# Stores of the gates, of FF1's first products and of its blocks and sums, issued by ScalarE and GpSimd in place of SyncE

## The chip, the core and the metric

The kernel runs on one core of a Trainium2 chip. The metric is the device time of one execution in microseconds (us). Every run compared here is one launch of the whole program. The engines are named as the profile names them: PE is TensorE, DVE is VectorE, ACT is ScalarE, POOL is GpSimd and SP is SyncE, which computes nothing and only issues transfers (DMAs).

## What is computed

One block of a streaming encoder, in fp32, for 1024 positions of width 1024:

```python
mod = silu(c) @ W_ada + b_ada                 # shift, scale, gate: twice
h = rms_norm(x) * (1 + scale1) + shift1
z = h @ W_in      # latents of q and kv, rotary key, input of the conv, 2 x 1024 gate logits
y_A = attention(z) @ W_o_mla                  # 8 heads, block-causal
y_B = conv_module(z)                          # GLU, depthwise conv (31), LayerNorm, swish, pointwise
x += gate1 * ((sigmoid(g_A) * y_A + sigmoid(g_B) * y_B) @ W_out)
h2 = rms_norm(x) * (1 + scale2) + shift2
x += gate2 * (relu(h2 @ W1) ** 2 @ W2)        # feed-forward, width 4096
```

## The kernel before

Each fp32 operand of a product is split into a high and a low part (`split`: a copy that rounds, mostly on ACT at line 108, then a subtraction on DVE or POOL at line 114), and each product is three matmuls (`mm`, line 117): high by high, low by high, high by low.

The stages, by the times of the profiled execution: adaLN, norm and h until 75 us; the GLU, the conv and the gates from 75 to 290; latents, keys and queries to 440, with the last gates between them; attention to 625; its output product to 700; W_out, the second norm and FF1's "first blocks" to 835; FF1's main loop to 1090; FF2 to the end.

Three groups of results that the change touches go to DRAM and back:

- The **gates** (`gate`, lines 405 to 409): each of the 16 blocks of 128 logits is a product of PE; ACT takes the sigmoid of each half from PSUM into a tile `sg`, and the half is stored to DRAM: 32 stores of 256 KB.
- FF1's **first products** (`first_block`, lines 1025 to 1032). FF1 is done by blocks with seven products where a plain 2 by 2 block scheme has eight. Products 1 and 2 of a block row m are computed ahead of the others for 12 of the 16 m. Product 1 is copied by ACT into a tile `p` and stored (`p1d`); product 1 plus product 2 is the block f11, which goes through ReLU and square on ACT (lines 1006 and 1007) and is stored (`fd`).
- FF1's **blocks and sums**. The main loop runs over the 16 m. For each, `prepare_w` loads two weight tiles p and q of 512 KB (line 891, tile `wraw`, two buffers for p) and forms sums and differences of their halves on DVE (lines 973, 974, 985, 986) and their splits (ACT: `hi`, `whi`, `s4h`; DVE: `lo`, `wlo`, `s4l`). PE runs products 3 to 7, DVE adds them up out of PSUM (`sum_of`, line 1015, tiles `u`), ACT squares f12, f21 and f22. `right_operands` (lines 1034 to 1050) loads f11 again (line 1037) and forms, on POOL, four sums T3, T1, T2, T4 (lines 1040, 1042, 1045, 1049), which FF2 needs as right operands. `keep` (line 1011) stores f22, f21 and the four sums: six stores of 256 KB for each m.

All 751 DMAs of the kernel are issued by SP, in one order. A framework builds that order, and the order of each engine, from the code and from its own forecast of the times; buffers and semaphores are its work too. An instruction waits where it stands for what it needs; what stands behind it on the same engine waits with it. So a store at the head of SP's queue, whose data is not there yet, holds the loads behind it.

Of the kernel before, what the change touches and what calls it, by code (L numbers as in the profile page):

```python
# [75 lines left out]
def block_kernel(ctx: ExitStack, tc: tile.TileContext, a: dict, out: bass.AP):  # L76
    nc = tc.nc
# [22 lines left out]
    def cs(c):  # L100
        return slice(c * C, (c + 1) * C)
# [4 lines left out]
    def copy(eng, o, i):  # L106
        if eng is nc.scalar:
            eng.activation(o, i, AF.Copy)  # L108
        else:
            eng.tensor_copy(o, i)  # L110
# [49 lines left out]
    d = first[4]  # L160
# [234 lines left out]
    def z_tile():  # L395
        return gemm(weights(), halves(h_hi), halves(h_lo), KD)

    s_d = [dram.tile([P, S], F32, name=f"sg{d}") for d in range(2 * KD)]
# [5 lines left out]
    def gate(d, new):  # L404
        o = z_tile()
        for c in range(2):
            s_t = new("sg")
            nc.scalar.activation(s_t, o[c], AF.Sigmoid)  # L408
            nc.sync.dma_start(s_d[d][:, cs(c)], s_t)

    def gates(n, new):
        for d in range(first[n], first[n + 1]):
            gate(d, new)
# [4 lines left out]
    with tc.tile_pool(name="cv", bufs=1, **right) as cv:  # L418
# [48 lines left out]
        for d in range(GA):  # L467
            gate(d, cv_half)
        conv(2, us[2])
        for d in range(GA, FILL[0]):  # L470
            gate(d, cv_half)
# [81 lines left out]
    with tc.tile_pool(name="lat", bufs=1, **left) as lat:  # L553
# [138 lines left out]
        d = first[4]  # L692
# [146 lines left out]
    def big(name, dt=F32):  # L839
# [4 lines left out]
    f_d = {n: [dram.tile([P, C], F32, name=f"fd{n}_{t}") for t in range(FF // P // 2)]  # L844
           for n in ("11", "21", "22", "T1", "T2", "T3", "T4")}
# [149 lines left out]
    def product(n, w):  # L995
        wk, bk = PRODUCTS[n]
        wh, wl = w[wk]
        o = bank()
        for i, (bh, bl) in enumerate(gb_[bk]):
            mm(o, wh[:, blk(i)], bh, i == 0, False)  # L1000
            mm(o, wh[:, blk(i)], bl, False, False)
            mm(o, wl[:, blk(i)], bh, False, i == 3)
        return o

    def square_relu(f):
        nc.scalar.activation(f, f, AF.Relu)  # L1006
        nc.scalar.activation(f, f, AF.Square)
        return f

    def keep(n, m, t):  # L1010
        nc.sync.dma_start(f_d[n][m], t)

    def sum_of(x, y):
        t = small("u")
        last_sum[0] = nc.vector.tensor_tensor(t, x, y, ALU.add)  # L1015
        return t

    p1 = {}
    last_sum = [None]
    p1_d = [dram.tile([P, C], F32, name=f"p1d{m}") for m in range(NPRE)]  # L1020

    def p1_tile(name):
        return small_pool.tile([P, C], F32, name=name, tag="p1", bufs=NP1)

    def first_block(m, w):
        p1[m] = p1_tile("p1")
        copy(nc.scalar, p1[m], product(1, w))
        if m < NPRE:
            nc.sync.dma_start(p1_d[m], p1[m])
        u = sum_of(product(2, w), p1[m])  # L1030
        keep("11", m, square_relu(u))
        return last_sum[0]

    def right_operands(m, f12, f21, f22):

        f11 = p1_tile("f11")
        nc.sync.dma_start(f11, f_d["11"][m])
        keep("22", m, f22)
        t3 = p1_tile("t3")
        nc.gpsimd.tensor_tensor(t3, f22, f12, ALU.subtract)  # L1040
        keep("T3", m, t3)
        nc.gpsimd.tensor_tensor(f12, f12, f11, ALU.subtract)
        keep("T1", m, f12)
        t2 = p1_tile("t2")
        nc.gpsimd.tensor_tensor(t2, f22, f12, ALU.subtract)
        keep("T2", m, t2)
        keep("21", m, f21)
        t4 = p1_tile("t4")
        nc.gpsimd.tensor_tensor(t4, f21, t2, ALU.subtract)
        keep("T4", m, t4)  # L1050

    NP = FF // P // 2
    rest = right_blocks()
# [1 line left out]
    for m in range(NPRE):  # L1055
        sums.append(first_block(m, first_row(m)[1]))
        if m >= 3:
            with tc.issue_after(sums[m - 1].ins):
                for _ in range(2):
                    next(rest, None)  # L1060
# [3 lines left out]
    for m in range(NP):  # L1064
        nxt = prepare_w(m + 1) if m + 1 < NP else None
        if m >= NPRE:
            first_block(m, w)
        if m == NP - 1:
            gap.close()
            w2a = ctx.enter_context(tc.tile_pool(name="w2a", bufs=1, **left))  # L1070
        ps = {n: product(n, w) for n in ((5, 3, 6, 7, 4) if m == 0 else (6, 7, 5, 3, 4))}
        if m < NPRE:
            p1[m] = small_pool.tile([P, C], F32, name="p1r")
            nc.sync.dma_start(p1[m], p1_d[m])
        u2 = sum_of(ps[6], p1[m])
        u3 = sum_of(ps[7], u2)
        f22 = square_relu(sum_of(ps[5], u3))
        u4 = sum_of(ps[5], u2)
        f12 = square_relu(sum_of(ps[3], u4))
        f21 = square_relu(sum_of(ps[4], u3))  # L1080
        right_operands(m, f12, f21, f22)
        w = nxt
# [222 lines left out]
```

## Time and profile before

| | |
|---|---|
| median of three runs | 1402.04 us (1401.58 to 1405.19) |
| the profiled execution: its own time | 1403.63 us |
| its span in the profile | 1401.5 us |
| PE busy | 1335.7 us, 95% of the span |
| DVE, ACT, POOL busy | 71%, 49%, 29% |
| DMA queue of SP | 49.3% of 16 engines' span |

The span is the time from the first to the last instruction that the profile shows; the execution's own time is 2.1 us longer. PE is the engine to watch: what does not lengthen or shorten its 66 us of idle time does not move the end. The engines' shares are means over stages that differ, so each place of the change has to be read by itself.

### The profile page before, as it was taken

How to read it: one execution, taken by the hardware profiler on the slowest of the kernel's cores; microseconds unless marked ns; L12 is line 12 of the kernel's file. 1: busy time of each engine (PE TensorE's matmuls, PEld its weight loads, DVE VectorE, ACT ScalarE, POOL GpSimd, SP SyncE). 2: the span in 40 equal slices, each digit the busy share in tenths (PEclk: the TensorE clock that was granted, in tenths of full speed). 3: DMA queues.
4: the chain of work that ended last, by engine and by line, in shares of the span. 5: the costliest groups of instructions: out<-in, count | busy, mean ns of one | idle time of the engine just before them, and what ended most of it. 6: DMA issues, size and time to landing. Idle time of an engine off the chain costs nothing. (4 is left out here: it accounts for less than half of the span.)

```text
span 1401.5 us, 17857 instructions
## 1 busy us (share of the span) xinstructions
PE 1335.7 (95%) x6160; PEld 1088.4 (78%) x6160; DVE 995.6 (71%) x1488; ACT 680.4 (49%) x1107; POOL 402.2 (29%) x280
## 2 busy tenths in 40 slices
PE   3899999999998999999999999989999999999998
PEld 2687888887676888878788878767778887887787
DVE  7969997955346788767546788766675459848854
ACT  6345422246556777753345763343455444444342
POOL 0049932244554655425100003334333100000000
PEclk9999999999999999999999999999999999999999
DMA  9611227731475323127546555566656678633442
GB/s 358 218 45 53 84 93 277 260 121 60 137 253 188 121 91 121 47 77 259 190 135 205 188 186 208 197 195 210 211 176 234 236 227 279 215 98 90 140 139 76
DMA packets 106186, 234.72 MB, mean 167 GB/s; under 512 B 12016, under 2 KB 12272, under 8 KB 106096
## 3 DMA queue, kind: packets, MB, share of 16 engines
q1 hardware_dynamic: 106096, 233.58, 49.3%
q8 instruction: 48, 0.79, 0.2%
q14 instruction: 42, 0.34, 0.1%
HBM read 169.57 MB, written 63.96 MB: 167 GB/s over the span
## 5 line engine op out<-in xcount | busy, mean ns | idle before, releaser
L117 PE MATMUL z<-hhi,whi 128*128 128x512 f32 x384 | 152.7, 399 | 0.4 <-ACT sg L408 0.4
L117 PE MATMUL z<-hlo,whi 128*128 128x512 f32 x384 | 152.4, 397 | 0.0
L117 PE MATMUL z<-hhi,wlo 128*128 128x512 f32 x384 | 152.1, 397 | 0.0
L1040 POOL TENSOR_TENSOR t<-u 128x512 f32<-128x512 f32 x16 | 23.0, 1440 | 316.4 <-DMA wraw<-in_w_ff 171.4
L108 ACT ACTIVATE whi<-wraw 128x1024 fp32r<-128x1024 f32 x71 | 74.9, 1055 | 59.7 <-PE z L117 46.4
L453 DVE SCALAR_TENSOR_TENSOR k<-u,vec,k 128x1024 f32<-128x1024 f32 x84 | 100.9, 1281 | 0.0
L114 POOL TENSOR_TENSOR wlo<-wraw,whi 128x1024 fp32r<-128x1024 f32 x25 | 62.6, 2503 | 115.0 <-ACT whi L108 110.3
L117 PEld LDWEIGHTS z<-hhi,whi 128*128 128x128 f32 x384 | 72.3, 188 | 19.6 <-ACT sg L408 1.0
L117 PEld LDWEIGHTS z<-hhi,wlo 128*128 128x128 f32 x384 | 72.3, 188 | 18.2
L117 PEld LDWEIGHTS z<-hlo,whi 128*128 128x128 f32 x384 | 72.4, 188 | 17.4
L114 DVE TENSOR_TENSOR wlo<-wraw,whi 128x1024 fp32r<-128x1024 f32 x46 | 60.7, 1319 | 26.2 <-ACT whi L108 26.2
L282 DVE CUSTOM_DVE_ANT_0 wada<-wada,c_act,vec 128x1024 f32<-128x1024 f32 x48 | 66.0, 1410 | 7.8 <-DMA wada<-in_w_ada 7.8
L1006 ACT ACTIVATE u<-u 128x512 f32<-128x512 f32 x64 | 39.9, 628 | 63.1 <-DVE u L1015 61.2
L446 POOL TENSOR_TENSOR accp<-accp,prc 128x1024 f32<-128x1024 f32 x28 | 67.4, 2413 | 9.8 <-ACT prc L445 8.6
L117 PE MATMUL z<-ghT,hi 128*128 128x512 f32 x160 | 62.9, 393 | 1.7 <-DVE u L1015 1.7
L117 PE MATMUL z<-glT,hi 128*128 128x512 f32 x160 | 62.5, 391 | 0.0
L117 PE MATMUL z<-ghT,lo 128*128 128x512 f32 x160 | 62.3, 390 | 0.0
L117 PE MATMUL z<-l_whi,h_whi 128*128 128x512 f32 x148 | 57.9, 391 | 4.1 <-DVE l_whi L114 4.1
L1015 DVE TENSOR_TENSOR u<-z,u 128x512 f32<-128x512 f32 x80 | 52.9, 684 | 10.4 <-PE z L117 7.2
L117 PE MATMUL z<-l_wraw,h_wraw 128*128 128x512 f32 x152 | 59.6, 392 | 0.0
L117 PE MATMUL z<-h_wraw,l_wraw 128*128 128x512 f32 x152 | 59.2, 390 | 0.0
L117 PE MATMUL z<-l_wlo,h_wlo 128*128 128x512 f32 x148 | 57.7, 390 | 0.1
(363 smaller groups left out, 3893.8 us busy)
## 6 DMA issues: line engine op xcount, KB each, us to landing
wada<-in_w_ada SPq DMA_DIRECT2D x48, 512.0 KB, 5.9
wraw<-in_w_ff SPq DMA_DIRECT2D x44, 512.0 KB, 4.2
fraw<-fdT SPq DMA_DIRECT2D x64, 256.0 KB, 2.7
wraw<-in_w_in SPq DMA_DIRECT2D x24, 512.0 KB, 3.6
fd<-u SPq DMA_DIRECT2D x48, 256.0 KB, 2.6
fdT<-t SPq DMA_DIRECT2D x48, 256.0 KB, 4.3
fraw<-fd SPq DMA_DIRECT2D x48, 256.0 KB, 2.8
w<-in_w_ff SPq DMA_DIRECT2D x48, 256.0 KB, 3.8
```

The source lines that it names most:

```text
L108: eng.activation(o, i, AF.Copy)
L114: lo_eng.tensor_tensor(lo, src, hi.bitcast(F32), ALU.subtract)
L117: nc.tensor.matmul(o, l, r, start=start, stop=stop)
L282: nc.vector.tensor_tensor_reduce(out=w, in0=w, in1=c_act, scale=1.0, scalar=v("b_ada", j), op0=ALU.mult, op1=ALU.add, accum_out=dst,)
L446: nc.gpsimd.tensor_tensor(accp, accp, pr, ALU.add)
L453: nc.vector.scalar_tensor_tensor(t, u[:, j:j + S], w(j), t, ALU.mult, ALU.add)
L1006: nc.scalar.activation(f, f, AF.Relu)
L1015: last_sum[0] = nc.vector.tensor_tensor(t, x, y, ALU.add)
L1040: nc.gpsimd.tensor_tensor(t3, f22, f12, ALU.subtract)
```

## The change

The issuing engine of 156 stores changes; what is stored, where and out of which buffer stays. ACT issues the 32 stores of the gates, the 12 of the first products, and those of f11, f22 and f21 (16 each): 92. POOL issues the 64 stores of T3, T1, T2 and T4. SP keeps every load and the other stores.

```diff
@@ def gate(d, new):
             nc.scalar.activation(s_t, o[c], AF.Sigmoid)
-            nc.sync.dma_start(s_d[d][:, cs(c)], s_t)
+            nc.scalar.dma_start(s_d[d][:, cs(c)], s_t)
@@
-    def keep(n, m, t):
-        nc.sync.dma_start(f_d[n][m], t)
+    def keep(n, m, t, eng=nc.scalar):
+        eng.dma_start(f_d[n][m], t)
@@ def first_block(m, w):
         if m < NPRE:
-            nc.sync.dma_start(p1_d[m], p1[m])
+            nc.scalar.dma_start(p1_d[m], p1[m])
@@ def right_operands(m, f12, f21, f22):
-        keep("T3", m, t3)
+        keep("T3", m, t3, nc.gpsimd)
         nc.gpsimd.tensor_tensor(f12, f12, f11, ALU.subtract)
-        keep("T1", m, f12)
+        keep("T1", m, f12, nc.gpsimd)
@@
-        keep("T2", m, t2)
+        keep("T2", m, t2, nc.gpsimd)
@@
-        keep("T4", m, t4)
+        keep("T4", m, t4, nc.gpsimd)
```

The order of the instructions shows what this does on the engines. A row is a line of the kernel, the operation, and what it writes and reads.

**The latents.** On ACT, at 330 us: two sigmoids of a gate (`sg`), the rounding copy of a weight tile (`whi`), then the load of another table of functions and the root `rl` of the latents' norm, for which PE waits. Before:

```order
L408 ACTIVATE sg<-z 128x512
L108 ACTIVATE whi<-wraw 128x1024
L408 ACTIVATE sg<-z 128x512
L212 ACT_TABLE_LOAD
L212 ACTIVATE rl<-rl_ms 128x8
```

With the change:

```order
L408 ACTIVATE sg<-z 128x512
L108 ACTIVATE whi<-wraw 128x1024
L409 DMA sg_638<-sg 128x512
L408 ACTIVATE sg<-z 128x512
L409 DMA sg_638<-sg 128x512
L212 ACT_TABLE_LOAD
L212 ACTIVATE rl<-rl_ms 128x8
```

Both stores of the gate now stand ahead of the table load and of `rl`, the second directly behind the sigmoid whose result it stores.

**The first blocks.** On ACT, at about 800 us: the copy of product 1 (`p`), ReLU and square (lines 1006 and 1007), the rounding copies of weights (`whi`) and of the operands (`gh`, `ghT`). Before:

```order
L1006 ACTIVATE u<-u 128x512
L108 ACTIVATE gh_3_7613<-x_7_6026 128x512
L108 ACTIVATE p_7623<-z 128x512
L108 ACTIVATE ghT_0_7658<-x_4_6023 128x512
L108 ACTIVATE ghT_1_7663<-x_5_6024 128x512
L108 ACTIVATE ghT_2_7805<-x_2_6021 128x512
L108 ACTIVATE ghT_3_7809<-x_3_6022 128x512
L108 ACTIVATE whi<-wraw 128x1024
L1007 ACTIVATE u<-u 128x512
```

With the change:

```order
L1006 ACTIVATE u<-u 128x512
L108 ACTIVATE p_7623<-z 128x512
L108 ACTIVATE ghT_0_7658<-x_4_6023 128x512
L1011 DMA fd_5_6040<-u 128x512
L108 ACTIVATE ghT_1_7663<-x_5_6024 128x512
L108 ACTIVATE ghT_3_7809<-x_3_6022 128x512
L108 ACTIVATE whi<-wraw 128x1024
L1007 ACTIVATE u<-u 128x512
L1029 DMA p1d_7276<-p_7623 128x512
L1006 ACTIVATE u<-u 128x512
```

A store of f11 (`fd`) now stands two operations ahead of the next `whi`, and a store of product 1 (`p1d`) between the square and the next ReLU.

**FF1's main loop.** On SP, one m and a half: `wraw` are the weight loads, `p1r` loads product 1 back, `f` is the load of f11, and `fd` and `fdT` are the stores of blocks and sums. Before:

```order
L891 DMA wraw<-in_w_ff 128x1024
L1011 DMA fd_7_6074<-u 128x512
L891 DMA wraw<-in_w_ff 128x1024
L1011 DMA fdT_7_6122<-t_8850 128x512
L1011 DMA fd_7_6058<-u 128x512
L1011 DMA fdT_7_6090<-u 128x512
L1074 DMA p1r<-p1d_7278 128x512
L1011 DMA fdT_7_6106<-t_8855 128x512
L1037 DMA f_8968<-fd_8_6043 128x512
L1011 DMA fdT_7_6138<-t_8859 128x512
```

With the change, two m:

```order
L891 DMA wraw<-in_w_ff 128x1024 x2
L1074 DMA p1r<-p1d_7277 128x512
L1037 DMA f_8847<-fd_7_6042 128x512
L891 DMA wraw<-in_w_ff 128x1024 x2
L1074 DMA p1r<-p1d_7278 128x512
L1037 DMA f_8968<-fd_8_6043 128x512
```

SP is left with the four loads of an m. On POOL, with the change, the same m:

```order
L1040 TENSOR_TENSOR t_8850<-u 128x512
L1011 DMA fdT_7_6122<-t_8850 128x512
L1042 TENSOR_TENSOR u<-u,f_8847 128x512
L1011 DMA fdT_7_6090<-u 128x512
L1045 TENSOR_TENSOR t_8855<-u 128x512
L1011 DMA fdT_7_6106<-t_8855 128x512
L1049 TENSOR_TENSOR t_8859<-u,t_8855 128x512
L1011 DMA fdT_7_6138<-t_8859 128x512
```

Each sum of POOL is followed by its own store, where the four sums stood back to back before. On ACT, the store of f22 now stands between its square and the ReLU of f12, and the store of f21 behind its square, at the end of the m's work.

## Rows read from the trace of the kernel before

**Rows 1.** The page: span, and TensorE's busy time, share and instructions.
```profile
span 1401.5 us, 17857 instructions
...
PE 1335.7 (95%) x6160; PEld 1088.4 (78%) x6160; DVE 995.6 (71%) x1488; ACT 680.4 (49%) x1107; POOL 402.2 (29%) x280
```

**Rows 2.** Chain of waits, TensorE, whole span: total us, times, longest us.
```profile
PE z L117 <- DVE u L1015: 8.3, 9, 1.9
```

**Rows 3.** Waits of SyncE's queue, whole span, same columns.
```profile
SPq L409 <- ACT sg L408: 112.4, 27, 14.0
SPq L1011 <- ACT u L1007: 71.9, 30, 6.3
```

**Rows 4.** Timeline of ScalarE at the gates: start, length, instruction, idle before.
```profile
219.75 0.60 ACT L408 ACTIVATE sg<-z 128x512 f32<-128x512 f32 x1 [9.21 <-issue]
```

**Rows 5.** Windows: length; busy PE, PEld, DVE, ACT, POOL; clock, DMA share, GB/s.
```profile
225.00:250.00 25.00, 25.00 (x122) 20.54 (x120) 20.74 (x28) 5.10 (x8) 5.79 (x2) 1.00 1.01 388
800.00:825.00 25.00, 24.56 (x107) 19.65 (x106) 23.38 (x35) 21.08 (x36) 0.00 (x0) 1.00 0.63 210
```

**Rows 6.** Timeline of ScalarE, latents.
```profile
331.50 0.58 ACT L408 ACTIVATE sg<-z 128x512 f32<-128x512 f32 x1
332.09 1.28 ACT L212 ACT_TABLE_LOAD   x1
```

**Rows 7.** Timeline of TensorE, the same place.
```profile
334.60 1.55 PE L236 MATMUL c<-ident,rl 128*128 128x128 f32 x8 [1.63 <-DVE rl L216]
```

**Rows 8.** Timeline of SyncE, first blocks (first and last of ten stores).
```profile
801.48 0.32 SPq L1029 DMA_DIRECT2D p1d<-p  x1
...
820.96 0.32 SPq L1029 DMA_DIRECT2D p1d<-p  x1
```

**Rows 9.** Line 891, the loads of FF1's weights.
```profile
L891 SPq DMA_DIRECT2D wraw<-in_w_ff x44: 327/333/458, 748.2 to 1041.5; - x44
...
DMA to landing us min/median/max: 3.5/4.2/6.2
```

**Rows 10.** Timeline of SyncE, one m of FF1's main loop.
```profile
961.51 0.33 SPq L891 DMA_DIRECT2D wraw<-in_w_ff  x1
961.93 0.38 SPq L1011 DMA_DIRECT2D fdT<-t  x1
962.41 0.38 SPq L1011 DMA_DIRECT2D fd<-u  x1
```

**Rows 11.** Timeline of VectorE, the same m.
```profile
960.12 1.36 DVE L114 TENSOR_TENSOR s4l<-wraw,s4h 128x512 fp32r<-128x512 f32 x1 [1.29 <-ACT s4h L108]
...
965.71 0.69 DVE L973 TENSOR_TENSOR wy<-wraw 128x512 f32<-128x512 f32 x1 [3.63 <-DMA wraw<-in_w_ff]
...
967.65 0.68 DVE L1015 TENSOR_TENSOR u<-z,u 128x512 f32<-128x512 f32 x1
```

**Rows 12.** Timeline of TensorE, the same m.
```profile
968.39 0.50 PE L117 MATMUL z<-ghT,whi 128*128 128x512 f32 x1 [1.42 <-DVE u L1015]
```

**Rows 13.** Six windows of 25 us, 900 to 1050: their sum.
```profile
sum 150.00, PE 140.92 PEld 110.74 DVE 101.38 ACT 63.52 POOL 56.17; mean PE 23.49 PEld 18.46 DVE 16.90 ACT 10.59 POOL 9.36
```

**Rows 14.** Timeline of ScalarE, the same m.
```profile
960.64 0.64 ACT L1007 ACTIVATE u<-u 128x512 f32<-128x512 f32 x1
967.77 1.06 ACT L108 ACTIVATE hi<-wraw 128x1024 fp32r<-128x1024 f32 x1 [6.49 <-DVE wraw L985]
...
973.05 0.63 ACT L1006 ACTIVATE u<-u 128x512 f32<-128x512 f32 x1 [1.03 <-DVE u L1015]
```

**Rows 15.** Timeline of GpSimd, the same m: first and last operation.
```profile
959.64 1.29 POOL L1040 TENSOR_TENSOR t<-u 128x512 f32<-128x512 f32 x1 [9.16 <-ACT u L1007]
...
964.09 1.29 POOL L1049 TENSOR_TENSOR t<-u,t 128x512 f32<-128x512 f32 x1
```

**Rows 16.** The page: a group of GpSimd, and a group of DMAs to landing.
```profile
L114 POOL TENSOR_TENSOR wlo<-wraw,whi 128x1024 fp32r<-128x1024 f32 x25 | 62.6, 2503 | 115.0 <-ACT whi L108 110.3
...
fdT<-t SPq DMA_DIRECT2D x48, 256.0 KB, 4.3
```

## The prediction

> **What bounds the kernel now.** I read the page first. PE is busy for 1335.7 of 1401.5 us [rows 1], so 66 us of its idle time are all that a shorter program could give back. The waits of PE come next: none of them names a store or any DMA of this change. The only one inside FF1's main loop is for DVE's sums u, 9 times and 8.3 us in all [rows 2]. The waits of SP's queue look very different: it stands 112.4 us at stores of the gates and 71.9 us at stores of ReLU-squares [rows 3]. These waits are what the change removes, so the question is which load behind them was late, and whether PE needed it.
>
> **What leaves SP.** At the gates, the stores hold back the loads of the adaLN weights. There the transfers fill the 16 DMA engines anyway (share 1.01 between 225 and 250 us), and PE is busy 25.00 of 25 us [rows 5]. An earlier issue brings nothing there: 0.
>
> In FF1's main loop the load that matters is p. Its buffer comes free when `s4l` ends, at 960.12 + 1.36 = 961.48, and SP issues the load at 961.51 [rows 10, 11]. So the load waits for no store that stands ahead of it in the queue. It lands for DVE at 965.71, 4.20 us after the issue. DVE then forms the sums of the halves, and the u that empties PE's bank stands behind them, from 967.65 on. PE resumes at 968.39, after 1.42 us idle [rows 11, 12]. The path of an m is therefore: `s4l`, p's transfer, DVE, PE; SP's issue is not in it. What can still change is the length of the transfer. The median of this line is 4.2 us, the shortest 3.5, the longest 6.2 [rows 9]. Behind p on the same queue come the store of T3 0.42 us later and that of f21 0.90 us later [rows 10]. With the change, T3's store goes to POOL and may start later, which helps p. The store of f21 is issued by ACT as soon as its square ends, at 960.64 + 0.64 = 961.28 [rows 14], so ahead of p rather than behind it, and p1r and f follow p without a gap on SP. The two moves oppose each other. The bounds for an m are -0.7 (all at 3.5) and +2.0 (all at 6.2). I take +0.2, since one store moves ahead of p and one moves away, and since the median is nearer to the short end. Times the 9 m that wait: **+1.8 us** (bounds -6.3 and +18).
>
> The Trainium skill ("DMA: Bandwidth & Descriptors", section "Issuing engines are not separate DMA queues") says that DMAs from the scalar, sync or gpsimd engine end on the same 16 engines and interleave, so that issuing from several saves sequencer time only. By that rule this term is 0 and the gates' too. The rows agree as far as they go: the load that matters does not wait for SP's sequencer.
>
> **What comes to ACT: 92 issues.** The trace has no DMA issued by ACT. The nearest rows are SP's own, 0.32 to 0.38 us for a store [rows 8, 10]. A store that stands right behind its producer also waits for the producer's end. I take 0.3 to 0.5 us each. What counts is what stands behind it.
>
> - *Gates, 75 to 290 us.* ACT is idle for 9.21 us ahead of a sigmoid [rows 4]. Two stores are hidden in this. Some also wait for a counter that SP's loads share, and then for a load of up to some us; that fits into the same gap: 0.
> - *Latents.* The second sigmoid ends at 331.50 + 0.58 = 332.08 and the table load starts at 332.09 [rows 6]; PE stands idle for 1.63 us until 334.60, waiting for the root behind it [rows 7]. ACT has no gap, so the two stores of sg_638 go straight onto PE's path: 2 x 0.32 is 0.64. I take **+0.6** (bounds 0.3, if the first hides, and 1.0). The other gates between the latents stand behind other waits: 0.
> - *First blocks.* Between 800 and 825 us ACT is busy 21.08 us of 25, DVE 23.38, and PE loses 0.44 [rows 5]. Ten stores fall into this stretch [rows 8]: 3.2 to 5.0 us of issue for 3.9 us of idle ACT. At most 1.1 us stay over there. The stretches around it are looser. I take **+1.0** for all of the first blocks. The lower bound is 0 (stores that stand a few operations behind their producer cost ACT only a gap that it has), the upper one 24 x 0.32 = 7.7, with all 24 that fall here on PE's path.
> - *Main loop.* Behind the square of f22, ACT idles 1.03 us until the ReLU of f12, waiting for DVE; behind the square of f21 it idles 6.49 us until `hi` [rows 14]. A store of 0.38 hides in either. If the cover went, f12's ReLU would be later, then f12's square and `s4h`, which stands behind that ReLU, then `s4l` and the next p: up to 0.4 us for each m.
>
> **What comes to POOL: 64 issues.** POOL's four sums of an m run from 959.64 to 964.09 + 1.29 = 965.38, 5.74 us, after 9.16 us idle [rows 15]. A period is thus 14.9 us. With four issues of c us, POOL becomes the bound where 5.74 + 4c exceeds 14.9, at c = 2.3. No row has a DMA of POOL. The bounds are 0.32 (SP's issue) and 2.5 (POOL's longest operation of this kind [rows 16]). I take 1.0, nearer to SP's issue, because it moves no data itself: 9.7 us of 14.9, hidden. f12's buffer, which T1 leaves, comes free with T1's store, and stores of sums take 4.3 us to land [rows 16]; two more us there stay within the 9 us gap: 0.
>
> **The sum**: 0 + 1.8 + 0.6 + 1.0 = +3.4 us. On the profiled execution (1403.63, its span plus 2.1) that is 1407.0; this execution lies 1.6 above the median of 1402.04. Against the median I forecast **1405.4 us**.
>
> **The rivals.**
> 1. *Faster: p's transfer gets short.* p no longer shares its queue with stores, and every bound m gets 3.5 us in place of 4.2. Nine times 0.7 is 6.3; less 1.6 for latents and first blocks: 1397.3. For it: SP is left with four loads an m, and the whole loss of PE from 900 to 1050 is 150 - 140.92 = 9.1 us [rows 13], which has room for this. Against it: the same bytes move in the same time, and T3's store starts behind p already.
> 2. *Slower: POOL becomes the bound.* At c = 2.5 a period is 15.7 us in place of 14.9, 0.8 more, times 16 m is +13; with the other terms 1418. It decides from c = 2.3. For it: POOL's own operations are slow (2.5 us [rows 16]). Against it: an issue of SP takes an eighth of that. The Trainium skill ("SBUF — State Buffer", section "SBUF: two separate sides", the trap that DVE blocks DMA) has the descriptors of GpSimd's DMAs written by GpSimd itself, which is locked out while DVE holds the port that both share; its section "A bandwidth-pool intuition that's wrong" gives 3.1 us in place of 0.62 for one transfer beside such an operation. It names copies in DVE's faster modes; the rows of DVE in this m are sums of two tensors [rows 11], and no run here has such a store yet.
> 3. *Slower: ACT in the first blocks.* If the 24 stores of that stretch lie on PE's path, or wait there for loads whose counter they share: 7.7 in place of 1.0, that is 1412. For it: ACT and DVE are the fullest there [rows 5]. Against it: PE's own loss in this stretch is only 0.44.
> 4. *No change at all.* SP's waits hid nothing, ACT's stores find gaps everywhere: 1402.
>
> **How the numbers follow.** Within 0.3% (4.2 us), a measurement of this kernel can't tell a change from none; that is 1397.8 to 1406.2. My forecast with rival 4, which give small sums of either sign, gets 0.52 (0.02 faster, 0.38 same, 0.12 slower). Rival 1 gets 0.20 (0.18 faster, 0.02 same), rival 2 gets 0.14 (slower), rival 3 gets 0.14 (0.04 same, 0.10 slower). Together: faster 0.20, same 0.44, slower 0.36. The range reaches from just below rival 1 to rival 2: 1395 to 1418. The forecast's own range is 1400 to 1410.
>
> **What would show it.** SP's waits for `sg` and for the squares disappear, and PE's busy time stays. At the latents, the idle time of 1.63 grows to about 2.2. Between 800 and 825, ACT's free time is used up and PE's loss grows by up to 1.1. In the main loop, the time from p's issue to DVE's next sum shows whether it is 4.2, 4.4 or 3.5; the idle time of POOL ahead of T3's sum shows c: 9.16 less 4c. The forecast is wrong if p's transfer moves by more than 0.5 us in most m, if c exceeds 2.3, or if ACT waits at a store for a load while PE waits for ACT.

## The result, and the profile after

The change makes the kernel slower: 1411.74 us (median of 4 runs, 1409.15 to 1413.51) against 1401.9; the ratio is 1.0061, with a 95% interval of 1.0040 to 1.0081. By that ratio it is 8.6 us more (the two medians differ by 9.8), where 3.4 more was forecast. The time lies inside the range of 1395 to 1418, but outside the forecast's own 1400 to 1410; the 8.6 us are twice what I had called the bound to no change. The profiled execution has a span of 1411.6 us, 10.1 more than before.

The page after, with the span, the busy times and two new queues:

```profile
span 1411.6 us, 17796 instructions
...
PE 1335.0 (95%) x6160; PEld 1087.7 (77%) x6160; DVE 1004.6 (71%) x1488; ACT 681.1 (48%) x1107; POOL 428.3 (30%) x344
...
q10 hardware_dynamic: 13248, 24.12, 4.6%
q0 software_dynamic: 5120, 16.78, 3.1%
```

PE is as long busy as before [rows 1], so over the whole span the 10 us are idle time. The stores of ACT go through a hardware queue of their own (q10), those of POOL through a software queue (q0). Where PE idles is told by its waits over the whole span:

```profile
PE z L117 <- DVE u L1015: 15.4, 8, 2.8
...
PE c L236 <- DVE rl L216: 2.0, 1, 2.0
```

The wait for DVE's sums u was 8.3 us before [rows 2] and is 15.4 now. The windows show the same place. First the two stretches of [rows 5], then the sum of the six windows from 900 to 1050:

```profile
225.00:250.00 25.00, 25.00 (x117) 20.40 (x117) 19.89 (x28) 5.13 (x8) 5.17 (x2) 1.00 0.99 385
800.00:825.00 25.00, 24.52 (x107) 19.66 (x106) 23.45 (x36) 20.85 (x37) 0.00 (x0) 1.00 0.64 208
```

```profile
sum 150.00, PE 132.33 PEld 103.87 DVE 97.60 ACT 60.35 POOL 69.25; mean PE 22.06 PEld 17.31 DVE 16.27 ACT 10.06 POOL 11.54
```

At the gates PE is busy 25.00 of 25 us as before; in the first blocks it loses 0.48 us (0.44 before), with ACT no fuller. In FF1's main loop it loses 150 - 132.33 = 17.7 us, against 9.1 before [rows 13]: 8.6 us more, as much as the ratio gives. Timed from the first `wy` to the last sum u, the stage takes 271.2 us in place of 261.4, which is 9.8 of the 10.1 us by which the span grew. What the idle time leaves over fits TensorE's granted clock. PE waits some 2 us in each m here (2.07 us until 956.29), and two of the six windows show less than 1.00, where the kernel before has 1.00 in all six:

```profile
950.00:975.00 25.00, 20.87 (x85) 16.10 (x84) 15.47 (x21) 8.22 (x11) 11.41 (x13) 0.96 0.58 203
975.00:1000.00 25.00, 24.26 (x101) 19.06 (x101) 15.55 (x20) 10.42 (x16) 11.62 (x13) 0.97 0.52 181
```

These are means: for a part of the two windows the clock stood at the lower of its two levels, 1.2 GHz in place of 2.4. By the means, 4% and 3% of 25 us are 1.7 us.

One m of the main loop shows how it comes about. POOL first:

```profile
945.91 1.29 POOL L1040 TENSOR_TENSOR t<-u 128x512 f32<-128x512 f32 x1 [7.73 <-ACT u L1007]
947.50 0.56 POOL L1011 DMA_DIRECT2D fdT<-t  x1 [0.30 <-POOL t L1040]
...
952.44 1.30 POOL L1049 TENSOR_TENSOR t<-u,t 128x512 f32<-128x512 f32 x1
...
962.33 1.29 POOL L1040 TENSOR_TENSOR t<-u 128x512 f32<-128x512 f32 x1 [7.73 <-ACT u L1007]
```

Each store keeps POOL for 0.56 us and waits 0.30 us for the sum to end. T4's sum, the last, now ends 952.44 + 1.30 - 945.91 = 7.83 us after T3's began; before it was 5.74 [rows 15]. The next m begins at 962.33, 16.42 us after this one. Now SP (p's load), the store of f21 on ACT, and DVE:

```profile
947.78 0.33 SPq L891 DMA_DIRECT2D wraw<-in_w_ff  x1
```

```profile
947.56 0.33 ACTq L1011 DMA_DIRECT2D fd<-u  x1
```

```profile
946.38 1.37 DVE L114 TENSOR_TENSOR s4l<-wraw,s4h 128x512 fp32r<-128x512 f32 x1 [1.29 <-ACT s4h L108]
...
953.35 0.95 DVE L973 TENSOR_TENSOR wy<-wraw 128x512 f32<-128x512 f32 x1 [5.00 <-DMA wraw<-in_w_ff]
...
955.55 0.68 DVE L1015 TENSOR_TENSOR u<-z,u 128x512 f32<-128x512 f32 x1
```

The load of p is issued at 947.78, 0.03 us after `s4l` has ended, and lands for DVE at 953.35, after 5.57 us (4.20 before). (What I call p's load, here and in the prediction, is by the code q's: `wy` at line 973 adds the two halves of q, and q goes into the buffer that p of the m before leaves when `s4l` ends. The times and waits read from it stay the same.) But the sum `wy` that DVE begins then takes 0.95 us, where it took 0.69 [rows 11]; the sum u at 955.55, for which PE waits, comes later by as much. `wy` begins while POOL still forms T4's sum, and ends 0.56 us after it: 954.30 against 953.74.

### The profile page after: what moved, and what is told of

Same layout as the page of the kernel before. It is cut to its first block, busy times and chain, and to the rows that moved or that the text cites. A ratio compares the mean times of both kernels' runs of the same rounds, so it can differ in the third digit from the quotient of the medians.

```text
span 1411.6 us, 17796 instructions
## 1 busy us (share of the span) xinstructions
PE 1335.0 (95%) x6160; PEld 1087.7 (77%) x6160; DVE 1004.6 (71%) x1488; ACT 681.1 (48%) x1107; POOL 428.3 (30%) x344
```

## The experiments

When I had read only waits and landings, three theories stood. **A**: f21's store, on ACT's own queue and 0.22 us ahead of p's load, takes part of the transfer that p had to itself. **B**: POOL's stores do. **C**: p1r and f, which an emptied SP issues right behind p, do. In all three p's transfer is the loss. Each kernel ran beside the kernel before on the same chip. Its median there was 1404.4, 1404.8 and 1403.4 us in the three groups, so ratios are compared.

**Only POOL's stores.** The change with the 92 stores of ACT put back:

```diff
-            nc.scalar.dma_start(s_d[d][:, cs(c)], s_t)
+            nc.sync.dma_start(s_d[d][:, cs(c)], s_t)
...
-        keep("22", m, f22)
+        keep("22", m, f22, nc.sync)
...
-        keep("21", m, f21)
+        keep("21", m, f21, nc.sync)
```

> Only the 64 stores of T3, T1, T2, T4 are issued by GpSimd; all 92 others are SyncE's again. Theory A (f21's store, on ScalarE's own queue just ahead of p's load, shares the transfer time that p had to itself): p lands about 4.2 to 4.5 us after its issue, TensorE idles about 9 to 11 us between 900 and 1050, time about 1402 to 1404. Theory B (the stores of GpSimd, in a queue of their own, are what shares with p): p lands after about 5.5 us, TensorE idles about 17 us there, time about 1410. Theory C (p1r and f, issued straight behind p by an emptied SyncE): part of it, p about 4.8.

Measured: 1415.31 us, ratio 1.0082 (1.0067 to 1.0097). The whole loss is there with the 64 stores of POOL alone, so A is not needed for it. In the six windows PE loses 150 - 134.76 = 15.2 us:

```profile
sum 150.00, PE 134.76 PEld 105.98 DVE 104.20 ACT 61.56 POOL 70.41; mean PE 22.46 PEld 17.66 DVE 17.37 ACT 10.26 POOL 11.74
```

But p lands early, which B did not foresee:

```profile
981.59 0.33 SPq L891 DMA_DIRECT2D wraw<-in_w_ff  x1
...
982.50 0.41 SPq L1074 DMA_DIRECT2D p1r<-p1d  x1
983.00 0.68 SPq L1037 DMA_DIRECT2D f<-fd  x1
```

```profile
985.95 2.16 DVE L973 TENSOR_TENSOR wy<-wraw 128x512 f32<-128x512 f32 x1 [3.79 <-DMA wraw<-in_w_ff]
988.15 0.69 DVE L974 TENSOR_TENSOR wy<-wy,wraw 128x512 f32<-128x512 f32 x1
```

```profile
986.25 1.30 POOL L1049 TENSOR_TENSOR t<-u,t 128x512 f32<-128x512 f32 x1
```

Here p is in place at 985.95, 4.36 us after its issue, and `wy` begins at once, but takes 2.16 us. T4's sum runs from 986.25 to 987.55; `wy` ends at 988.11, again 0.56 us behind it. C is not needed either: p1r and f are issued 0.91 and 1.41 us behind p here, with a store between (0.60 and 1.03 in the change), and p lands early.

**Only ACT's stores.** The four `nc.gpsimd` of the change put back to `nc.sync`, the other 92 stores left with ACT.

> The 92 stores of ScalarE as in the change; T3, T1, T2, T4 are SyncE's again. Theory A: p lands about 5.5 us after its issue and the time is about 1410. Theory B: p about 4.2 to 4.4, time about 1402 to 1404, with only the small losses at the latents and the first blocks left. Theory C: about 4.2, since the four sums are back between the loads.

Measured: 1403.91 us, ratio 1.0005 (0.9992 to 1.0017): nothing, so the price of ACT's 92 issues can't be told from zero. On A it says little: the framework orders the sums of DVE otherwise in this kernel, and f21's store then stands 2.0 to 3.5 us ahead of p's load, where it stood 0.22 ahead in the change.

**ACT's stores without the main loop.** Gates, first products and f11 with ACT; f22, f21 and the sums back on SP.

> Gates, first products and f11 are stored by ScalarE as in the change; f22, f21 and the four sums are SyncE's again, so that the main loop of FF1 issues almost as before. All theories of the main loop: p about 4.2 us, TensorE idles about 9 us between 900 and 1050. What is left is the price of the latents and the first blocks: my prediction has +1.6 us there (bounds 0.3 to 8.7), so 1403.5; the trace of the change shows 0.4 at 334 us and nothing between 725 and 850, so 1402 to 1403.

Measured: 1404.81 us, ratio 1.0001 (0.9988 to 1.0014). The latents and the first blocks cost nothing that a measurement can tell; the trace of the change shows what there is. ACT at the latents, then PE:

```profile
332.00 0.33 ACTq L409 DMA_DIRECT2D sg<-sg  x1
332.35 1.28 ACT L212 ACT_TABLE_LOAD   x1 [0.39 <-ACT sg L408]
```

```profile
334.84 1.94 PE L236 MATMUL c<-ident,rl 128*128 128x128 f32 x8 [1.99 <-DVE rl L216]
```

The second store stands between the sigmoid and the table load for 0.35 us; the first hid behind the copy of the weights. PE's idle time grows from 1.63 [rows 7] to 1.99.

**f21's store behind p.** The change with one edit, `keep("21", m, f21, nc.sync)`.

> The change with one edit: the 16 stores of f21 are SyncE's again, where they stand behind p's load. Theory A: p goes back to 4.2 to 4.5 us and the time to about 1403. Theory B: p stays at about 5.5 and the time at about 1410. Theory C: p1r and f now stand one store further behind p: p about 5.2, time about 1408.

Measured: 1414.29 us, ratio 1.0075 (1.0052 to 1.0098). In its trace p's load is issued at 947.78, at the same time as in the change, and DVE has p at 952.40, 0.95 us earlier than there:

```profile
947.78 0.33 SPq L891 DMA_DIRECT2D wraw<-in_w_ff  x1
948.21 0.39 SPq L1011 DMA_DIRECT2D fd<-u  x1
```

```profile
952.40 1.90 DVE L973 TENSOR_TENSOR wy<-wraw 128x512 f32<-128x512 f32 x1 [4.05 <-DMA wraw<-in_w_ff]
954.33 0.69 DVE L974 TENSOR_TENSOR wy<-wy,wraw 128x512 f32<-128x512 f32 x1
```

`wy` now takes 1.90 us and ends at 954.30, the time at which it ended in the change. So A is right about p (4.6 us in place of 5.6 with the store behind it), and wrong that p's landing sets the end of `wy`. It comes close, though: in the change, with p at 953.35, a `wy` of 0.69 us would have ended at 954.04, only 0.26 us ahead of the real one. So f21's store by itself might have cost most of the same time; no run here has it ahead of p without POOL's sums beside `wy`. That gave theory **D**: a sum of DVE whose two inputs lie in SBUF does not end before a sum of POOL that it meets. The next four kernels try it.

**No store moved, POOL's sums longer.** The kernel before, with T2's sum formed three times:

```diff
-        nc.gpsimd.tensor_tensor(t2, f22, f12, ALU.subtract)
+        for _ in range(3):
+            nc.gpsimd.tensor_tensor(t2, f22, f12, ALU.subtract)
```

> The kernel before, with every store on SyncE; GpSimd forms each T2 three times in place of once, which puts 2.7 us of its sums ahead of T4's, about as much as the stores did. No transfer is changed. Theory D (VectorE's sums of two tiles in SBUF are held while GpSimd forms a sum, so that the wy of the next m can't end before T4's sum has): the chain of GpSimd's sums ends about 8.5 us after it began, wy lasts 1.4 to 2.2 us in place of 0.69, a period of m is about 16.4 us in place of 14.8, TensorE idles 15 to 18 us between 900 and 1050, time about 1411 to 1415. Theory B (the stores of GpSimd share the transfer time with p): nothing of the kind, 1402 to 1405 and 9 us idle.

Measured: 1419.46 us, ratio 1.0108 (1.0082 to 1.0135), without any change of a transfer. POOL and DVE in one m:

```profile
969.67 1.62 POOL L1042 TENSOR_TENSOR u<-u,f 128x512 f32<-128x512 f32 x1
971.36 4.02 POOL L1046 TENSOR_TENSOR t<-u 128x512 f32<-128x512 f32 x3
975.46 1.62 POOL L1050 TENSOR_TENSOR t<-u,t 128x512 f32<-128x512 f32 x1
```

```profile
970.06 0.68 DVE L1015 TENSOR_TENSOR u<-z,p1r 128x512 f32<-128x512 f32 x1
974.52 1.41 DVE L973 TENSOR_TENSOR wy<-wraw 128x512 f32<-128x512 f32 x1 [3.79 <-DMA wraw<-in_w_ff]
975.97 1.67 DVE L974 TENSOR_TENSOR wy<-wy,wraw 128x512 f32<-128x512 f32 x1
```

Two sums of DVE are held in turn: the first ends at 975.93, 0.55 us after the repeated T2 (975.38), the second at 977.64, 0.56 us after T4 (977.08). From the first one's begin to the second one's end it is 3.12 us; in the next kernel, where nothing holds them, 1.41. The sum u at 970.06, with one input in PSUM, lies wholly beside T1's sum and keeps its 0.68 us. From 850 to 1075 us, over the whole of the loop, PE idles 225 - 208.30 = 16.7 us, 9.1 in the kernel before:

```profile
850.00:1075.00 225.00, 208.30 (x863) 164.38 (x862) 159.47 (x181) 90.60 (x132) 120.18 (x82) 0.97 0.57 184
950.00:975.00 25.00, 21.61 (x83) 17.07 (x82) 14.39 (x18) 9.14 (x14) 14.78 (x11) 0.86 0.64 196
```

That is 7.6 of the 14.7 us that the run lost. Behind waits of up to 3.4 us TensorE's granted clock fell as well: 0.97 over this stretch, 0.86 in the window 950 to 975, against 1.00 in all six windows of the kernel before; 3% of 225 us are 6.8 more. The hold works in both directions: T1's and T4's sums take POOL 1.62 us here, each behind a held sum of DVE, where they take 1.30 in the change. B forecast no change here; whether it adds to the loss where POOL does store, the next kernel tells.

**POOL's stores without T4's sum:** `t4` and its sum taken out, `keep("T4", m, t2, nc.gpsimd)` in their place, all else as in the kernel with only POOL's stores.

> The kernel with only GpSimd's 64 stores moved, without T4's sum: T2's tile is stored in T4's place, so the part of the output that comes from T4 is another. All four stores of an m stay on GpSimd. Theory D: the last sum, T2's, ends about 5.7 us after the first begins, before p lands; wy lasts 0.69 again, a period is about 15 us, TensorE idles 8 to 10 us between 900 and 1050, time 1402 to 1406. Theory B: four stores as before this edit, so about 1415 and 15 us idle.

Measured: 1402.59 us, ratio 0.9984 (0.9967 to 1.0000), PE's loss 150 - 143.45 = 6.5 us. All four stores of an m still go through POOL. The last sum there, and `wy`:

```profile
962.59 1.30 POOL L1045 TENSOR_TENSOR t<-u 128x512 f32<-128x512 f32 x1
```

```profile
964.58 0.69 DVE L973 TENSOR_TENSOR wy<-wraw 128x512 f32<-128x512 f32 x1 [3.90 <-DMA wraw<-in_w_ff]
965.30 0.69 DVE L974 TENSOR_TENSOR wy<-wy,wraw 128x512 f32<-128x512 f32 x1
```

The sum ends at 963.89, before p lands, and `wy` takes 0.69. With the same four stores, PE's loss is 6.5 us where it was 15.2, so B falls.

**Sums first, then stores.** In the code the four sums stand ahead of the four stores; on POOL a store then stands one sum behind the sum that it stores.

```diff
-        keep("T3", m, t3, nc.gpsimd)
...
+        for n, t in (("T3", t3), ("T1", f12), ("T2", t2), ("T4", t4)):
+            keep(n, m, t, nc.gpsimd)
```

> The kernel with only GpSimd's 64 stores moved, with the code's order changed: the sums first, then the stores. On GpSimd one sum then stands between a sum and its store, so no store waits for the end of the sum ahead of it, and only two stores stand ahead of T4's sum in place of three. Theory D: T4's sum ends about 6.6 us after the first sum begins, in place of 7.85, at about the time p lands; wy is held by 0 to 0.5 us, a period is 15 to 15.4 us, TensorE idles 9 to 12 us between 900 and 1050, time 1403 to 1408. Theory B: the same bytes in the same queue, so about 1415.

Measured: 1406.42 us, ratio 1.0019 (1.0001 to 1.0036), PE's loss 8.4 us. The stores no longer wait 0.30 us for their sum:

```profile
960.60 0.56 POOL L1011 DMA_DIRECT2D fdT<-t  x1
961.18 1.30 POOL L1043 TENSOR_TENSOR t<-u 128x512 f32<-128x512 f32 x1
...
962.99 1.30 POOL L1046 TENSOR_TENSOR t<-u,t 128x512 f32<-128x512 f32 x1
```

```profile
963.72 1.13 DVE L973 TENSOR_TENSOR wy<-wraw 128x512 f32<-128x512 f32 x1 [3.62 <-DMA wraw<-in_w_ff]
```

T4's sum ends 6.6 us after the first began (964.29), p lands at 963.72, and `wy` is held for 0.44 us. With POOL's stores in all three, the hold of `wy` in the m shown is 0, 0.44 and 1.47 us (no T4 sum, sums first, only POOL's stores), and PE's loss 6.5, 8.4 and 15.2. The two smaller losses lie below the 9.1 of the kernel before, so the 0.19% of this kernel, which just clears the noise, is not found in PE's idle time.

**The sums on DVE.** The kernel before, stores on SP, with `nc.vector` for the four `nc.gpsimd` sums.

> The kernel before, with all stores on SyncE, and the four sums of an m formed by VectorE in place of GpSimd. Theory D: a sum of two tiles takes VectorE 0.69 us, four take 2.8 us of the 3.6 to 5 us in which it waits for p; s4l and wy are never held, s4l takes 0.68 in place of 1.36, p is issued 0.7 us earlier, a period is about 14 us, TensorE idles 3 to 7 us between 900 and 1050, time 1396 to 1400. Theory B: nothing held in the kernel before, so nothing to win there; VectorE gets 2.8 us more for each m, 1402 to 1408.

Measured: 1391.93 us, ratio 0.9918 (0.9890 to 0.9945); run again in the next group 1392.77, ratio 0.9919 (0.9892 to 0.9945). This beats the kernel before by 0.8%, some 11 us, and the change by more. DVE in one m, and the sum of the six windows:

```profile
947.67 0.69 DVE L114 TENSOR_TENSOR s4l<-wraw,s4h 128x512 fp32r<-128x512 f32 x1 [0.62 <-ACT s4h L108]
948.28 0.68 DVE L1040 TENSOR_TENSOR t<-u 128x512 f32<-128x512 f32 x1
...
950.98 0.69 DVE L1049 TENSOR_TENSOR t<-u,t 128x512 f32<-128x512 f32 x1
952.62 0.69 DVE L973 TENSOR_TENSOR wy<-wraw 128x512 f32<-128x512 f32 x1 [0.95 <-DMA wraw<-in_w_ff]
```

```profile
sum 150.00, PE 150.00 PEld 122.17 DVE 121.77 ACT 69.36 POOL 0.00; mean PE 25.00 PEld 20.36 DVE 20.30 ACT 11.56 POOL 0.00
```

The line of `s4l` over the whole run, in the kernel before and here (min, median and max, in ns):

```profile
L114 DVE TENSOR_TENSOR s4l<-wraw,s4h x16: 678/1276/1775, 831.1 to 1055.8; 128x512 fp32r<-128x512 f32 x16
```

```profile
L114 DVE TENSOR_TENSOR s4l<-wraw,s4h x16: 678/683/692, 831.6 to 1039.4; 128x512 fp32r<-128x512 f32 x16
```

`s4l` takes 0.69 us where it took 1.36 [rows 11], the four sums fit into the time in which DVE waits for p, `wy` takes 0.69, and PE does not idle at all in these windows. This fits a loss of the same kind in the kernel before, where `s4l` was held in 10 of 16 m and `wy` in 3. How much of the 11 us is the hold alone no run separates: the edit also takes the four sums out of POOL's longer time for them.

**The change with the sums on DVE**, and **all 156 stores on ACT with the sums on DVE**. The edits are those above, on the change.

> The change as it is, all 156 stores moved, with the four sums formed by VectorE; GpSimd only issues their stores. Theory D: nothing holds VectorE any more, so the loss of the change is gone although its 64 stores still go through GpSimd's queue: TensorE idles 0 to 4 us between 900 and 1050, time 1390 to 1396. If the stores themselves cost something (p at 5.4 us in place of 4.2, as the trace of the change shows), it stands at the upper end, 2 to 4 us above the kernel with SyncE's stores and VectorE's sums. Theory B: 1400 or more.

> All 156 stores on ScalarE, those of the four sums too, and the sums formed by VectorE. Theory D: 1390 to 1395, TensorE idle 0 to 3 us between 900 and 1050. If ScalarE's issues held up its own work (rival 3 of the prediction), the squares and s4h would come later by 0.3 to 0.5 us a store: 1396 or more.

> The kernel before with the four sums on VectorE and every store on SyncE, run again beside the other two on the same chip: 1390 to 1395. If moving the stores pays or costs anything of its own, once GpSimd forms no sums, it is the difference of the other two from this one; I expect 0 to 3 us more for the change.

Measured: 1391.77 us, ratio 0.9908 (0.9876 to 0.9941), and 1391.14, ratio 0.9908 (0.9877 to 0.9940). PE is busy 150.00 of 150 us in both. The intervals lie over that of SP's stores, 0.9919 (0.9892 to 0.9945): where the stores are issued makes no difference that can be told, once POOL forms no sums. In the first of the two POOL issues a store beside DVE's sums:

```profile
932.35 0.69 DVE L1042 TENSOR_TENSOR u<-u,f 128x512 f32<-128x512 f32 x1
...
932.61 0.54 POOL L1011 DMA_DIRECT2D fdT<-t  x1 [11.50 <-DVE t L1040]
933.34 0.54 POOL L1011 DMA_DIRECT2D fdT<-u  x1 [0.19 <-issue]
```

An issue takes 0.54 us there, no longer than the 0.56 of the change; DVE's sums did not hold it, nor it DVE's sum.

## Why the prediction was right, and which step failed

The range held the time and the direction came out, but that is luck in good part. Of the 3.4 us forecast, ACT's 1.6 measured 0.4, and p's 1.8 were covered by something else; the 8.6 us come from a term that I had put at 0. The range reached so high for rivals 2 and 3, which did not occur. Point by point:

- **What leaves SP: 0.** Right. At the gates nothing moved, and p's load is issued 0.03 us after its buffer is free in both kernels. SP's waits of 112 and 72 us hid nothing.
- **p's transfer: +0.2 us for each m.** Mis-sized. In the change it takes 5.57 us in place of 4.20; from 931 to 997 us, five m in a row, it takes 5.0 to 5.6 (4.2 to 4.5 there before), beyond the 0.5 us that I had named as a sign of a wrong forecast. Rival 1, a shorter p, went the other way. T3's store did not move away from p: POOL issues it at 947.50, 0.28 us ahead, so two stores overtake p and not one. With f21's behind p it takes 4.62, and the time does not move (the fourth experiment): the hold of `wy` ended later still and covered this term.
- **ACT's 92 issues: +0.6 and +1.0.** The latents measured +0.36, the first blocks +0.04 in PE's loss. The sum, 0.4, lies below what the runs resolve. Rival 3 is out: the 92 stores of ACT alone give 1.0005.
- **POOL's 64 issues: hidden, 0.** This step failed. c itself was nearly right: 0.56 us and 0.30 of waiting, 0.86, where I took 1.0. (The sign that I had named for it, 9.16 less 4c, misleads: POOL's 7.73 us would give 0.36, because the period grew as well.) Wrong was the cover: I held the 9.16 us of idle time behind T4's sum for free [rows 15]. But the cover of POOL is what lies between the end of T4's sum and the landing of p, 965.71 - 965.38 = 0.33 us [rows 11, 15]. The three stores ahead of T4 put 7.83 - 5.74 = 2.09 us there. From the first sum's begin, `wy` would end after 965.71 + 0.69 - 959.64 = 6.76 us and ends after 954.30 - 945.91 = 8.39 us: 1.63 us for each m on the path. The period confirms it: 16.42 us, where the rows of before give 5.74 + 9.16 = 14.90 [rows 15].
- **Rival 2** named the engine and the direction, but for another reason and with another threshold: POOL was never full (c = 0.86 against 2.3). Since `wy` takes 0.69 us itself and ends 0.56 behind T4's sum, by these rows it decides from about (0.33 + 0.13) / 3 = 0.15 us a store, an estimate.

I had the Trainium skill's page "SBUF — State Buffer", section "SBUF: two separate sides", in hand and read from it only the trap of GpSimd's descriptors. The same section says that DVE and GpSimd share a pair of ports which one instruction holds to its end, and that a DVE operation with two inputs in SBUF contends for it with a GpSimd operation that reads SBUF. I even wrote that the rows of DVE show sums of two tensors, and took that for an all-clear; by that rule it is the case that blocks. The traces agree: of DVE's sums, `wy` and `s4l` are held, and u, which has one input in PSUM, keeps 0.68 us beside POOL's sums (970.06 in the kernel with repeated sums). In one point they differ: the section gives the ports to whichever starts first, and with only POOL's stores `wy` begins at 985.95, 0.30 us ahead of T4's sum by the profile, and is held all the same. And the hint stood in my own rows: `s4l` took 1.36 us [rows 11], twice as long as `wy` of the same size, beside T3's sum [rows 15].

What stays open: why POOL's stores alone (1.0082) and the change with f21 behind p (1.0075) stand no lower than the change (1.0061); the intervals overlap. Open too is what f21's store ahead of p would cost without the hold. That a held sum of DVE ends 0.55 us after POOL's, and not at once, is seen in nearly every case but not explained; DVE's sums back to back begin 0.61 us apart (947.67 and 948.28 in the kernel with the sums on DVE), so it looks as if a held sum did its work only once POOL's had ended.

## What to carry to other kernels

An engine's idle time is not free cover if its instructions hold up another engine while they run: ask for each operation that is shifted what it will then run beside. Where two operations of one size and shape differ in length in a trace, find out why before anything is moved; here that row leads to a kernel that is 0.8 to 0.9% faster than the one before. Moving DMA issues off a queue brought nothing here, since no load on the path stood behind them; that is read from the gap between the release of its buffer and its issue, 0.03 us for p.

## What the runs showed of the hardware

- A sum of DVE on 128x512 fp32 with both inputs in SBUF takes 0.69 us alone. When it begins while a sum of POOL runs, it ends 0.54 to 0.56 us after that sum's end: `wy` at 0.95, 1.41, 1.67, 1.90 and 2.16 us in the rows above, and all but one of over 200 such meetings around the main loop, in the nine kernels in which POOL forms the sums. A sum of POOL that stands right behind a store of POOL holds DVE's also when that began up to 0.41 us ahead of it. Elsewhere a sum of DVE that began ahead of POOL's kept its 0.69 us, and POOL's could take longer instead: in the kernel before, `wy`'s second half at 877.54 and T3's sum at 877.58, 1.81 us in place of 1.29.
- A DVE sum with one input in PSUM is not touched: the sums u beside POOL's in the same traces take 0.67 to 0.69 us.
- A store of 256 KB costs POOL 0.54 to 0.56 us of issue (0.74 at most), and 0.30 us more behind the sum that it stores. The median is 0.33 us on ACT in the change (0.67 at most) and 0.32 on SP in the kernel before (1.7 at most).
- Two stores of 256 KB on queues of their own, T3's 0.28 us and f21's 0.22 us ahead of a load of 512 KB, went with a load of 5.57 us; with f21's behind the load on the load's own queue, and T3's still ahead, it took 4.62.
